# Moving two of eight depthwise-convolution tiles from TensorE to VectorE in a decoder step, with one spill and the mask conversions on other engines

## The chip, the core and the metric

The kernel runs on one core of a Trainium2 chip. The metric is the device time of one execution in microseconds (us). The core has four engines that compute: TensorE (PE in the rows, with its weight loads as PEld), VectorE (DVE), ScalarE (ACT) and GpSimd (POOL). SyncE (SP) issues transfers only; ScalarE and GpSimd issue transfers too, each from its own instruction queue. Each queue runs in order.

## What is computed

Two independent token streams pass the same two-layer trunk: a prompt of 512 tokens and a sample batch of 8 x 4 tokens. Only the prompt's part of the first layer is touched by the larger part of the change:

```python
a, g = split(h @ pw1_w + pw1_b, 2)          # D = 1024 channels
u = a * sigmoid(g)
full = concatenate([zeros(30, D), u])       # conv_prev is zero for the prompt
y = depthwise_conv(full, dw_w) + dw_b       # 31 taps for each channel, T = 512
y = silu(layer_norm(y)) @ pw2_w
```

After it come a squared-ReLU MLP, a K/V projection of the residual, stick-breaking attention (its causal mask is strict) and a second MLP. The sample goes through the same layers with a paged cache of 2048 past tokens.

## The kernel before

The prompt is held channel-major: 8 tiles of 128 channels x 512 tokens (index `kt` or `k`). Each dense product is made of three matmuls on a split of both operands into a rounded part and a rest (`whi`, `wlo` for weights, made by `wsplit`: ScalarE casts `whi` at L305, VectorE subtracts `wlo` at L306; two buffers each). The sample's dense products stream 1 MB weight blocks through four ring buffers, eight short matmul records to a block; its blocks are loaded from SP's queue.

The two streams are Python generators, `sample()` and `prompt()`. A loop at the end traces whichever has the smaller clock. Each yield adds a cost: a convolution tile 5.0 (`CV_COST`), a sample block 2.9 (`SMP_COST`); the sample starts at -20 (`CLK0`). A planner then gives each engine its fixed order: among the instructions that it takes to be ready it puts the one traced first ahead, by durations of its own; transposes and statistics of the norms (`Norm.add`) are moved ahead of others by 100 places.

The part around the change:

- The loop over `c` (four weight chunks) and `i` makes the gated tile `u` for `kt = 2c + i`: 48 matmuls, a sigmoid on ScalarE (L781), then `u` on VectorE (L785). GpSimd's queue writes `u` to the buffer `ud` in device memory behind 30 zero columns (L786); ScalarE copies the last 30 columns (L787). In the same loop the sample's gated tile and its own convolution (`sconv`, L705 and L707) run on VectorE, and the ada blocks of the sample (`early`, four to a tile from `c = 1`) on TensorE.
- `conv_load(k)` (L665) reads `ud[k]` back four times, shifted by one token each, into the 128 partitions of `raw[k]` (two buffers, four transfers of 270 KB from GpSimd's queue). The first two loads are traced in the loop above; `conv(k)` traces the load of `k + 2`.
- `conv(k)` makes `wk` on VectorE (L669), runs 32 matmuls of 128 x 32 in four column groups (L675; 64 records for a tile in the trace), adds the bias on ScalarE (L677) and gives the tile to the norm: four transposes (L351) and four statistics (L353).
- `prompt()` begins with the eight `conv(k)`, each with its yield of 5.0. Then the norm over all 1024 channels needs all eight tiles.
- `make_ax(v, 1, axd[1])`, after the first MLP, writes 8 scaled residual tiles on ScalarE (L469, in `tmp` buffers, of which there are four) and spills each to device memory from SP's queue (L471). It is traced just ahead of the K projection. The residual is read back after attention.
- Ahead of it the two attention masks are converted to bf16 in 8 copies of 64 x 128 on GpSimd (L1232); `maskx` needs a transfer of the causal tile (L1228). Attention reads the masks first at 1041.9 us.

Of the kernel before, what the change touches and what calls it, by code (L numbers as in the profile page):

```python
# [8 lines left out]
F32 = mybir.dt.float32  # L9
# [4 lines left out]
ALU = mybir.AluOpType  # L14
# [31 lines left out]
KTB = 2  # L46
STB = 3
LN_PRI = 100
CIN = 0
EIN = 4  # L50
CV_COST = 5.0
LN_COST = 16.0
# [59 lines left out]
def yoco_step_kernel(  # L112
# [353 lines left out]
    def make_ax(n, i, spill=None):  # L466
        for k in range(KT):
            t = n[k] if spill is None else tmp("axs")
            order(act(t, n[k], AF.Identity, scale=aln[:, i, k : k + 1], bias=aln[:, 4 + i, k : k + 1]), latest_act[-1])  # L469
            if spill is not None:  # L470
                dma(spill[k], t)  # L471

    def load_ax(i, k):
        t = tmp("axl")
# [184 lines left out]
    cnrm = Norm()  # L659
    raw = {}  # L660

    def conv_load(k):
        raw[k] = pld.tile([P, 4, T + 28], F32, tag="ur", bufs=2, name="ur")
        for j in range(4):
            pdma(raw[k][32 * j : 32 * j + 32], ud[k].rearrange("(g c) t -> c g t", g=4)[:, :, j : j + T + 28])  # L665

    def conv(k):
        wk = pld.tile([P, 32, 32], F32, tag="wk", bufs=2, name="wk")
        vec.tensor_tensor(wk, sel4.unsqueeze(1).to_broadcast([P, 32, 32]),  # L669
                          wtap[:, k, :].unsqueeze(2).to_broadcast([P, 32, 32]), op=ALU.mult)  # L670
        for ts in parts(H_CV and k == KT - 1):
            a = pm("cv")[:, 0 : ts.stop - ts.start]
            for m in range(8):
                for g in range(4):
                    mm(a[32 * g : 32 * g + 32, :], wk[:, 8 * g + m, :], raw[k][:, g, 4 * m + ts.start : 4 * m + ts.stop],  # L675
                       start=(m == 0), stop=(m == 7), tile_position=(0, 32 * g))
            act(y[k][:, ts], a, AF.Identity, bias=pcol(R_DWB, k))  # L677
            cnrm.add(y[k], k, ts)
        if k + 2 < KT:
            conv_load(k + 2)  # L680

    sy = sfm("sy", "sv", 2)

# [36 lines left out]
    for c in range(4):  # L720
# [48 lines left out]
        for i in range(2):  # L769
            kt = 2 * c + i  # L770
            if c:
                ws = [wsplit(st[o], i * P, P) for o in range(2)]
                accs = [pm("pw1") for _ in range(2)]
                for a, (whi, wlo) in zip(accs, ws):
                    for k in range(KT):
                        mm3(a, whi[:, k, :], wlo[:, k, :], hhi[k], hlo[k], k == 0, k == KT - 1)
                acc = accs
            else:
                acc = accs[2 * i : 2 * i + 2]
            sg = tmp("sg")  # L780
            act(sg, acc[1], AF.Sigmoid, bias=pcol(R_PWB + 1, kt))  # L781
            for _ in itertools.islice(early, EIN if c else 0):
                pass
            u = tmp("u")
            vec.scalar_tensor_tensor(u, acc[0], pcol(R_PWB, kt), sg, op0=ALU.add, op1=ALU.mult)  # L785
            pdma(ud[kt][:, CW - 1 : T + CW - 1], u)  # L786
            nc.scalar.copy(utail[:, kt, 0 : CW - 1], u[:, T - CW + 1 : T])  # L787
            if kt < 2:
                conv_load(kt)
            if kt < CIN:  # L790
                conv(kt)

    bq = base.tile([P, 8], F32, name="bq")
    for g in range(4):
# [361 lines left out]

    def prompt():

        for k in range(CIN, KT):
            conv(k)  # L1160
            yield CV_COST
        crow_ = ring("ucrow")[0:32, 0:D]
        for c in range(2):
# [65 lines left out]
        for t, src in ((maskw, ident), (maskx, causal)):  # L1229
            for hf in range(2):  # L1230
                for o in range(2):
                    nc.gpsimd.tensor_copy(t[hf * 64 : hf * 64 + 64, o, :], src[(hf ^ o) * 64 : (hf ^ o) * 64 + 64, :])  # L1232
        make_ax(v, 1, axd[1])
        kd = dr.tile([KT, P, T], F32, name="kd")
        vd = dr.tile([T, D], F32, name="vd")
# [212 lines left out]
```

## Time and profile before

| what | value |
|---|---|
| time, median of three runs | 1698.54 us (1697.76 to 1699.73) |
| the profiled execution | 1699.24 us |
| its span in the trace | 1697.5 us |
| TensorE busy | 1582.7 us, 93% of the span |
| VectorE busy | 918.8 us, 54% |
| ScalarE busy | 565.2 us, 33% |
| GpSimd busy | 196.0 us, 12% |
| convolution matmuls (L675) | 182 to 277 us of the span |

The profiled execution's time is 1.7 us longer than the span of its trace, and 0.7 us above the median of the runs. Busy times of TensorE are those of pipelined matmuls, so neighbouring records overlap, and a fully busy stretch need not be one at peak rate. A row of the timeline merges neighbours of one kind; in square brackets stand the idle time of the engine before it and what ended that.

### The profile page before, as it was taken

The numbers are of one execution on the slowest core, as the hardware profiler recorded it, in microseconds if no ns is written. First come the engines' busy times: TensorE is split into PE (matmuls) and PEld (weight loads), VectorE is DVE, ScalarE is ACT, GpSimd is POOL, SyncE is SP. The second block draws the span as 40 slices with busy tenths as digits, with TensorE's granted clock in tenths as the row PEclk, the third lists the DMA queues.
The fourth block names the chain that finished last, engine by engine and source line by source line (L and its number), as shares of the span: only waits on it lengthen the run. The fifth ranks groups of instructions, "written<-read, shape, count | busy, mean of one in ns | idle before, by whom it ended". The sixth has DMA issues, their size and how long they took to land.

```text
span 1697.5 us, 25694 instructions
## 1 busy us (share of the span) xinstructions
PE 1582.7 (93%) x10617; PEld 1095.9 (65%) x10617; DVE 918.8 (54%) x1744; ACT 565.2 (33%) x903; POOL 196.0 (12%) x239
## 2 busy tenths in 40 slices
PE   5899987989999999999989998988979999999995
PEld 2566422655777777777557865555767767557885
DVE  2465424566576655655563455986675434324446
ACT  1322103326222322333162253754172333223332
POOL 4110110100111211110011201021101000000002
PEclk9899999999999999999999999999999999999998
DMA  9798778969766866586879967364646495993221
GB/s 287 247 292 320 225 224 314 369 215 366 243 239 229 329 231 238 177 313 229 298 277 336 318 235 279 138 225 146 218 165 228 170 354 216 352 335 130 82 73 50
DMA packets 153769, 412.00 MB, mean 243 GB/s; under 512 B 8967, under 2 KB 82983, under 8 KB 129061
## 3 DMA queue, kind: packets, MB, share of 16 engines
q1 hardware_dynamic: 49891, 161.86, 26.1%
q0 software_dynamic: 24384, 151.81, 24.7%
q10 hardware_dynamic: 79378, 96.70, 17.4%
q8 instruction: 83, 1.36, 0.3%
q14 instruction: 33, 0.27, 0.1%
HBM read 392.78 MB, written 18.41 MB: 242 GB/s over the span
## 4 chain that ended last, share of the span: by engine, by line
PE 70%; issue 13%; DMA 9%; DVE 5%; ACT 2%; POOL 1%; ACTq 0%; DVEq 0%; POOLq 0%
PE pd L312 16%; PE pd L316 16%; PE pd L315 15%; PE cv L675 2%; PE sd_acc L536 2%; PE av L1029 2%; DMA kraw<-in_cache_k_dram,krow 2%; PE zt L978 2%; DMA stage<-in_conv_pw_w_dram 2%; PE pw L312 2%; PE pw L316 2%; PE pw L315 2%; DMA vt<-in_cache_v_dram,vrow 2%; DMA sw<-in_mlp_w_dram 2%; PE w_acc L563 1%
## 5 line engine op out<-in xcount | busy, mean ns | idle before, releaser
L306 DVE TENSOR_TENSOR wlo<-stage,whi 128x1024 fp32r<-128x1024 f32 x184 | 223.7, 1220 | 247.5 <-ACT whi L305 246.3
L305 ACT CAST whi<-stage 128x1024 fp32r<-128x1024 f32 x184 | 191.8, 1046 | 453.0 <-PE pd L316 378.9
L312 PE MATMUL pd<-xhi,whi 128*128 128x512 f32 (+1 forms) x832 | 317.8, 383 | 8.9 <-ACT whi L305 5.5
L315 PE MATMUL pd<-xhi,wlo 128*128 128x512 f32 (+1 forms) x832 | 315.4, 381 | 5.0 <-DVE wlo L306 4.6
L316 PE MATMUL pd<-xlo,whi 128*128 128x512 f32 (+1 forms) x832 | 309.3, 382 | 5.6 <-DVE xlo L445 4.4
L972 DVE STREAM_TRANSPOSE kt<-kraw 128x512 f32<-128x512 f32 x256 | 163.8, 686 | 104.4 <-DMA kraw<-in_cache_k_dram,krow 64.9
L312 PE MATMUL pd<-h2h,whi 128*128 128x512 f32 (+1 forms) x544 | 207.5, 388 | 2.1 <-DVE v L1147 1.6
L315 PE MATMUL pd<-h2h,wlo 128*128 128x512 f32 (+1 forms) x544 | 205.8, 382 | 0.0
L316 PE MATMUL pd<-h2l,whi 128*128 128x512 f32 (+1 forms) x544 | 204.6, 383 | 0.0
L312 PEld LDWEIGHTS pd<-xhi,whi 128*128 128x128 f32 x832 | 158.1, 190 | 59.7 <-ACT whi L305 14.8
L316 PEld LDWEIGHTS pd<-xlo,whi 128*128 128x128 f32 x832 | 155.0, 190 | 52.5 <-DVE xlo L445 9.7
L315 PEld LDWEIGHTS pd<-xhi,wlo 128*128 128x128 f32 x832 | 158.1, 190 | 46.1 <-issue 11.0
L1147 DVE SCALAR_TENSOR_TENSOR v<-pd,mod_B,v 128x512 f32<-128x512 f32 x120 | 87.2, 743 | 138.7 <-PE pd L316 138.3
L950 POOL DMA_INDIRECT kraw<-in_cache_k_dram,krow x64 | 65.7, 1026 | 604.4 <-DVE kt L972 404.7
L312 PEld LDWEIGHTS pd<-h2h,whi 128*128 128x128 f32 x544 | 102.0, 188 | 39.0 <-issue 12.1
L315 PEld LDWEIGHTS pd<-h2h,wlo 128*128 128x128 f32 x544 | 102.2, 188 | 28.4 <-issue 9.0
L316 PEld LDWEIGHTS pd<-h2l,whi 128*128 128x128 f32 x544 | 101.9, 188 | 26.5 <-issue 8.1
L1122 ACT ACTIVATE relu<-pd 128x512 f32<-128x512 f32 (+1 forms) x68 | 39.0, 573 | 236.2 <-PE pd L316 236.2
L950 POOL DMA_INDIRECT vt<-in_cache_v_dram,vrow x64 | 67.7, 1057 | 213.7 <-PE av L1029 176.2
L978 PE MATMUL zt<-kt,qb 128*32 128x128 f32 x2048 | 78.2, 280 | 9.2 <-DVE kt L972 8.4
L978 PEld LDWEIGHTS zt<-kt,qb 128*32 128x32 f32 x2048 | 53.8, 110 | 34.8 <-issue 17.9
L353 DVE BATCH_NORM_STATS2 bn<-lnT 128x6 f32<-128x128 f32 x160 | 36.6, 285 | 66.5 <-PE lnT L351 66.3
(295 smaller groups left out, 2015.7 us busy)
## 6 DMA issues: line engine op xcount, KB each, us to landing
sw<-in_mlp_w_dram SPq DMA_DIRECT2D x64, 1024.0 KB
stage<-in_mlp_w_dram ACTq DMA_DIRECT2D x64, 1024.0 KB
adaw<-in_ada_w_dram SPq DMA_DIRECT2D x40, 1024.0 KB
stage<-in_conv_pw_w_dram ACTq DMA_DIRECT2D x12, 1024.0 KB
ur<-ud POOLq DMA_DIRECT2D x32, 270.0 KB, 6.5
adaw<-in_ada_w_dram SPq DMA_DIRECT2D x16, 512.0 KB
swkv<-in_w_kv_dram SPq DMA_DIRECT2D x8, 1024.0 KB
stage<-in_w_kv_dram ACTq DMA_DIRECT2D x8, 1024.0 KB
```

Source lines behind the costliest of these rows:

```text
L305: nc.scalar.copy(hi, st[:, :, c0 : c0 + cw])
L306: vec.tensor_tensor(lo, st[:, :, c0 : c0 + cw], hi.bitcast(F32), op=ALU.subtract)
L312: first = mm(out, whi, xh, start=start, stop=False)
L315: mm(out, wlo, xh, start=False, stop=False)
L316: latest[:] = [mm(out, whi, xl, start=False, stop=stop)]
L353: vec.bn_stats(self.st[:, i, k, :], pt[:, i * P : i * P + P])
L536: mm(acc[32 * g : 32 * g + 32, :], hT[:, kk * 2 + kp, :], blk[:, kp * D + c * 512 : kp * D + c * 512 + 512], start=(kk == 0), stop=(kk == ...
L950: nc.gpsimd.indirect_dma_start(out=out, out_offset=None, in_=cache.rearrange("g (r e) h d -> (g r) (e h d)", e=2), in_offset=bass.Indirect ...
L972: ins = vec.transpose(kt[:, 2 * x : 2 * x + 2, :], raw[x].rearrange("p (e c) -> p e c", e=2)[:, :, c0 : c0 + 256])
L978: behind(mm(zt[u][32 * g : 32 * g + 32, f * P : f * P + P], qb[:, u, hh * 8 + bl].rearrange("p x q -> p (x q)"), kt[:, :, bl * 32 : bl * 3 ...
L1122: latest_act[:] = [act(r, a, AF.Relu)]
L1147: ins = vec.scalar_tensor_tensor(v[kt][:, ts], a, gt[:, kt, 8:9], v[kt][:, ts], op0=ALU.mult, op1=ALU.add)
```

## The change

Channel tiles 0 and 2 (`TAPS`) no longer go through `ud`, `conv_load` and TensorE. Their `u` is written by VectorE into a padded buffer `upad` in on-chip memory behind 30 zeroed columns. ScalarE makes tap 0 with the bias (`act`), and VectorE adds taps 1 to 30 one by one in place: 30 `scalar_tensor_tensor` instructions of 128 x 512 for a tile, each reading what the one before wrote. The tile then goes to the norm as before. The taps are a generator: five are traced behind each of the eight `u` tiles, and six behind each `conv(k)` of the six remaining tiles, until all 60 are out. The loads of `raw` follow the list of the six remaining tiles. `prompt()` yields its 5.0 six times in place of eight.

The spill of the residual (L471) is issued from ScalarE's queue in place of SP's. The 8 mask copies run on VectorE in place of GpSimd.

```diff
--- before.py
+++ after.py
@@ -46,7 +46,6 @@
 KTB = 2
 STB = 3
 LN_PRI = 100
-CIN = 0
 EIN = 4
 CV_COST = 5.0
 LN_COST = 16.0
@@ -468,7 +467,7 @@
             t = n[k] if spill is None else tmp("axs")
             order(act(t, n[k], AF.Identity, scale=aln[:, i, k : k + 1], bias=aln[:, 4 + i, k : k + 1]), latest_act[-1])
             if spill is not None:
-                dma(spill[k], t)
+                nc.scalar.dma_start(spill[k], t)
 
     def load_ax(i, k):
         t = tmp("axl")
@@ -659,6 +658,25 @@
     cnrm = Norm()
     raw = {}
 
+
+    TAPS = (0, 2)
+    REST = [k for k in range(KT) if k not in TAPS]
+    upad = {}
+
+    def conv_taps(k):
+        up = upad[k]
+        act(y[k], up[:, 0:T], AF.Identity, scale=prm[:, R_DW, k : k + 1], bias=pcol(R_DWB, k))
+        for j in range(1, CW):
+            vec.scalar_tensor_tensor(y[k], up[:, j : j + T], prm[:, R_DW + j, k : k + 1], y[k], op0=ALU.mult, op1=ALU.add)
+            yield
+        cnrm.add(y[k], k, ALL)
+
+    taps = itertools.chain(*[conv_taps(k) for k in TAPS])
+
+    def some_taps(n):
+        for _ in itertools.islice(taps, n):
+            pass
+
     def conv_load(k):
         raw[k] = pld.tile([P, 4, T + 28], F32, tag="ur", bufs=2, name="ur")
         for j in range(4):
@@ -676,8 +694,8 @@
                        start=(m == 0), stop=(m == 7), tile_position=(0, 32 * g))
             act(y[k][:, ts], a, AF.Identity, bias=pcol(R_DWB, k))
             cnrm.add(y[k], k, ts)
-        if k + 2 < KT:
-            conv_load(k + 2)
+        if k in REST[:-2]:
+            conv_load(REST[REST.index(k) + 2])
 
     sy = sfm("sy", "sv", 2)
 
@@ -781,14 +799,19 @@
             act(sg, acc[1], AF.Sigmoid, bias=pcol(R_PWB + 1, kt))
             for _ in itertools.islice(early, EIN if c else 0):
                 pass
-            u = tmp("u")
+            if kt in TAPS:
+                upad[kt] = pld.tile([P, T + CW], F32, tag="upad", bufs=len(TAPS), name="upad")
+                vec.memset(upad[kt][:, 0 : CW - 1], 0.0)
+                u = upad[kt][:, CW - 1 : T + CW - 1]
+            else:
+                u = tmp("u")
             vec.scalar_tensor_tensor(u, acc[0], pcol(R_PWB, kt), sg, op0=ALU.add, op1=ALU.mult)
-            pdma(ud[kt][:, CW - 1 : T + CW - 1], u)
+            if kt not in TAPS:
+                pdma(ud[kt][:, CW - 1 : T + CW - 1], u)
             nc.scalar.copy(utail[:, kt, 0 : CW - 1], u[:, T - CW + 1 : T])
-            if kt < 2:
+            if kt in REST[:2]:
                 conv_load(kt)
-            if kt < CIN:
-                conv(kt)
+            some_taps(5)
 
     bq = base.tile([P, 8], F32, name="bq")
     for g in range(4):
@@ -1156,8 +1179,9 @@
 
     def prompt():
 
-        for k in range(CIN, KT):
+        for k in REST:
             conv(k)
+            some_taps(99 if k == REST[-1] else 6)
             yield CV_COST
         crow_ = ring("ucrow")[0:32, 0:D]
         for c in range(2):
@@ -1229,7 +1253,7 @@
         for t, src in ((maskw, ident), (maskx, causal)):
             for hf in range(2):
                 for o in range(2):
-                    nc.gpsimd.tensor_copy(t[hf * 64 : hf * 64 + 64, o, :], src[(hf ^ o) * 64 : (hf ^ o) * 64 + 64, :])
+                    vec.tensor_copy(t[hf * 64 : hf * 64 + 64, o, :], src[(hf ^ o) * 64 : (hf ^ o) * 64 + 64, :])
         make_ax(v, 1, axd[1])
         kd = dr.tile([KT, P, T], F32, name="kd")
         vd = dr.tile([T, D], F32, name="vd")
```

## Rows read from the trace of the kernel before

**Rows 1.** The page: busy time by engine, and the chain that ended last.
```profile
PE 1582.7 (93%) x10617; PEld 1095.9 (65%) x10617; DVE 918.8 (54%) x1744; ACT 565.2 (33%) x903; POOL 196.0 (12%) x239
...
PE 70%; issue 13%; DMA 9%; DVE 5%; ACT 2%; POOL 1%; ACTq 0%; DVEq 0%; POOLq 0%
```

**Rows 2.** Two stretches: length, busy PE, PEld, DVE, ACT, POOL; granted clock, DMA share, GB/s.
```profile
85.00:182.00 97.00, 94.91 (x564) 66.83 (x563) 54.36 (x104) 22.01 (x40) 8.22 (x15) 0.98 0.88 302
182.00:279.00 97.00, 87.77 (x698) 27.52 (x697) 27.67 (x79) 10.20 (x17) 13.66 (x25) 0.96 0.79 239
```

**Rows 3.** The chain in order of time (start us, us, what), convolution matmuls.
```profile
182.22 6.15 PE cv L675 x56
...
188.71 5.27 PE cv L675 x42
```

**Rows 4.** TensorE's groups by line, 180 to 280 us: busy us, mean ns | idle before.
```profile
L675 PE MATMUL cv<-ur,wk 128*32 128x512 f32 x512 | 66.0, 611 | 4.5 <-DMA ur<-ud 4.5
L563 PE MATMUL w_acc<-sw,hT 128*32 128x512 f32 x112 | 16.5, 631 | 4.8 <-DMA sw<-in_mlp_w_dram 4.8
```

**Rows 5.** VectorE's groups by line and shape, whole span.
```profile
L1010 DVE SCALAR_TENSOR_TENSOR z_s<-z_s,fc,fx 128x512 f32<-128x512 f32 x16 | 11.3, 747 | 0.1
```

**Rows 6.** VectorE's timeline, two instructions of which the second reads the first.
```profile
287.00 0.68 DVE L405 TENSOR_TENSOR v<-v,mb 128x512 f32<-128x512 f32 x1
287.71 0.69 DVE L406 TENSOR_TENSOR v<-v,rb 128x512 f32<-128x512 f32 x1
```

**Rows 7.** Timelines of VectorE, then ScalarE, around the fifth and the seventh gated tile.
```profile
140.21 1.23 DVE L306 TENSOR_TENSOR wlo<-stage,whi 128x1024 fp32r<-128x1024 f32 x1 [0.18 <-ACT whi L305]
...
171.58 0.75 DVE L785 SCALAR_TENSOR_TENSOR u<-pw,prm,sg 128x512 f32<-128x512 f32 x1
172.24 1.22 DVE L306 TENSOR_TENSOR wlo<-stage,whi 128x1024 fp32r<-128x1024 f32 x1
...
146.43 1.06 ACT L305 CAST whi<-stage 128x1024 fp32r<-128x1024 f32 x1 [6.14 <-PE pw L316]
...
176.21 1.05 ACT L305 CAST whi<-stage 128x1024 fp32r<-128x1024 f32 x1 [3.63 <-PE pw L316]
```

**Rows 8.** Timelines of ScalarE and then SP's queue at the residual spill.
```profile
869.43 2.22 ACT L469 ACTIVATE axs<-v,aln 128x512 f32<-128x512 f32 x3
873.25 1.99 ACT L305 CAST whi<-stage 128x1024 fp32r<-128x1024 f32 x2 [1.60 <-PE pd L316]
...
876.72 0.41 ACTq L298 DMA_DIRECT2D stage<-in_w_kv_dram  x1
...
879.44 0.59 ACT L1242 COPY kT<-pd 128x512 f32<-128x512 f32 x1 [0.46 <-DMA axd<-axs]
...
870.26 9.06 SPq L471 DMA_DIRECT2D axd<-axs  x8
880.05 0.32 SPq L1243 DMA_DIRECT2D kd<-kT  x1
```

**Rows 9.** GpSimd's timeline around the mask copies.
```profile
840.29 1.36 POOL L1232 CAST maskw<-c 64x128 bf16<-64x128 f32 x4 [71.99 <-PE pd L316]
849.75 0.96 POOL L950 DMA_INDIRECT kraw<-in_cache_k_dram,krow  x1 [8.11 <-PE ada_A L238]
```

**Rows 10.** VectorE's copies of like size, by line, whole span.
```profile
L695 DVE COPY sfull<-stT 128x120 f32<-128x120 f32 x16 | 3.3, 276 | 3.8 <-PE stT L692 3.8
```

**Rows 11.** A group of VectorE's at the kernel's end; GpSimd's timeline beside it.
```profile
L1392 DVE SCALAR_TENSOR_TENSOR yt<-yt,mv,gb 128x512 f32<-128x512 f32 x4 | 6.0, 1544 | 0.0
...
1682.99 4.61 POOL L1390 TENSOR_TENSOR yt<-yt,gb 128x512 f32<-128x512 f32 x3
```

**Rows 12.** VectorE's and GpSimd's timelines at a load of the convolution's input.
```profile
189.77 1.23 DVE L669 TENSOR_TENSOR wk<-c,wtap 128x1024 f32<-128x1024 f32 x1 [0.17 <-PE cv L675]
...
190.03 2.21 POOL L665 DMA_DIRECT2D ur<-ud  x4 [5.60 <-PE cv L675]
```

**Rows 13.** Waits of SP's queue, 180 to 300 us: total, times, longest.
```profile
SPq L561 <- PE sd_acc L536: 30.6, 3, 29.7
```

## Prediction

> **What bounds the kernel now.** I read the page's busy times and the chain first, then the two stretches that the change touches, then single rows. TensorE is busy for 93% of the span and carries 70% of the chain that ended last; VectorE is busy for 54% [rows 1]. So time is gained where TensorE work leaves and nothing later takes its place. While the gated tiles are made (85 to 182 us) TensorE is busy for 94.9 of 97 us and VectorE for 54.4; in the convolution (182 to 279 us) it is 87.8 of 97 against 27.7 [rows 2]. The chain runs through the convolution's matmuls themselves [rows 3], so they are on the path. The 9.2 us that TensorE is not busy there are two waits for transfers: 4.5 us for a refill of the convolution's input and 4.8 us for the sample's weight blocks [rows 4].
>
> **What the change takes from TensorE.** 56 records of a convolution tile took 6.15 us and 42 took 5.27 us [rows 3], 98 in 11.42 us or 0.1165 us each; 64 make a tile, 7.46 us. Busy time would say 66.0 / 8 = 8.25 us [rows 4], but neighbouring records overlap. I take 7.46: two tiles are 14.9 us off the path (16.5 at most). The transposes for the norm stay. With the tiles go two yields of 5.0: when the last convolution tile is traced, the sample has been given (20 + 30) / 2.9 = 17.2 blocks in place of (20 + 40) / 2.9 = 20.7. These 3.4 blocks, 1.2 us of TensorE each (16.5 us for 112 records, eight to a block, [rows 4]), are not saved; they fall into later stretches. So the convolution should become shorter by about 14.9 + 4 = 19 us, and the kernel by 14.9 before costs. The transfers lose two writes of 256 KB and eight reads of 270 KB, 2.6 MB, and GpSimd's queue ten issues; nothing waits for that queue otherwise, so I count no gain, but it is the reason to keep open that the 9.3 us of waits shrink.
>
> **What the change adds on VectorE.** An instruction of the taps' kind and shape with all operands in on-chip memory took 747 ns [rows 5]. Each tap reads the one before; such a pair started 0.71 us apart for a first instruction of 0.68 us [rows 6], 0.03 more than its length. So a tap is 0.78 us, 60 are 47 us, five are 3.9 us. The two `wk` that go (1.23 us each, [rows 12]) are 2.5 us less. In the first stretch 40 taps take 31 us of VectorE's 42.6 free ones, in the second 20 take 15.6 of 69 [rows 2]: there is room. The last 20 are traced behind the first four of six tiles, so the last tap should be done two tiles ahead of the norm. Room on average is not cover at each place, though. What is queued behind five taps is the next `wlo`, which TensorE waits for: it was traced later, so the planner puts the taps ahead. The tightest of the six such places: `u` at 171.58, `wlo` from 172.24 to 173.46; it is wanted when the accumulation ahead of it ends, at 176.21, where the next cast is released [rows 7]. That is a margin of 2.7 us against 3.9 us of taps: 1.2 us late. The next tightest of the other five is `wlo` ready at 141.44 and wanted at 146.43 [rows 7], 5.0 us, which covers the burst. Cost taken: 1.2 us; between nothing, if the planner starts `wlo` first, and 6 us, if the later places slip by as much each. Tap 0 on ScalarE replaces the bias on ScalarE: nothing, since ScalarE is busy for 10 of 97 us there [rows 2].
>
> **The spill.** SP's eight issues sit between 870.26 and 879.3 us, each waiting for its tile; what follows on SP's queue at 880.05 waits for `kT`, not for them [rows 8]. So SP's queue gives nothing back. On ScalarE each issue takes some 0.41 us (the weight load at 876.72), eight are 3.3 us, in a stretch where ScalarE runs from the spilled tiles to the casts of the next weights and to `kT` without much rest [rows 8]; behind the issues wait those casts, for which TensorE waits in turn. Three tiles with three issues fit ahead of the cast of 873.25, which TensorE releases: 869.43 + 2.22 + 1.2 = 872.9. The other five issues lie ahead of `kT` and delay it by up to 2 us. I take 1.0 us, between 0 and 3.3. The Trainium skill says in "DMA: Bandwidth & Descriptors", section "Issuing engines are not separate DMA queues", that transfers issued from different engines share the same DMA engines, so that another issuer saves the issue time alone; by that the move has nothing to gain in landing times, and with all of the issue time on the path the sum would be 1688.6. No row here shows the spill from the other queue.
>
> **The masks.** On GpSimd the first four took 1.36 us after a wait of 72 us, and what stood behind them, a gather at 849.75, waited for a ring buffer [rows 9]; so GpSimd's queue held nothing up. On VectorE, copies of like size took 0.28 us [rows 10], eight 2.2 us, at the norm ahead of the K projection, where TensorE waits for VectorE. They are traced behind the norm and fill gaps of its chain; I take 0.5 us, between 0 and 2.2. The masks are needed at attention, long after.
>
> **Sum.** 1699.24 - 14.9 + 1.2 + 1.0 + 0.5 = 1687.0 for an execution like the profiled one, which is 0.7 us above the median of the runs: 1686.
>
> **The rivals.**
> A, the sample's chain starts late. Five taps behind the last `u` and six behind the first convolution tile are traced ahead of, or among, the sample's small dependent VectorE steps at 185 to 209 us. 11 x 0.78 = 8.6 us later would be the matmuls that free the ring, for which the first block of the sample's MLP waits (SP's longest wait there is 29.7 us, [rows 13]); TensorE, in order, then waits in front of a block. For it: both transfer waits of this stretch are of that family [rows 4]. Against: those steps were traced before the convolution's taps, so only five taps lie ahead for sure, and TensorE has convolution tiles to fill with. It leaves 1686 + 8.6 = 1695. The planner putting the 20 late taps at the end of the convolution, so that the norm waits, comes out about there too.
> B, the waits go. With 2.2 MB less of refills in the convolution both waits of 9.3 us vanish: 1686 - 9.3 = 1677. For it: a refill is what the 4.5 us waited for [rows 4]. Against: six tiles in less time ask for the four refills that are left at the same pace as before, and the mean share of the transfers is 0.79 already [rows 2].
> C, slower: VectorE becomes the bound of the first stretch. At the end of the kernel four instructions of this very kind and shape took 1.54 us each on average, while GpSimd computed beside them [rows 11]; the 747 ns are from where it does not. At 1.54 us 40 taps with their gaps are 63 us on top of 54.4: 117 for 97, 20 more, and 1686 + 20 = 1706. It decides from a tap with its gap of (97 + 14.9 - 54.4) / 40 = 1.44 us on; from (97 - 54.4) / 40 = 1.07 to there it only eats the gain. Against: GpSimd does nothing but issue transfers there, and an instruction with two on-chip operands beside such an issue kept its 1.23 us [rows 12]. The Trainium skill states in "SBUF — State Buffer", section "Who interferes with whom", that a VectorE instruction with two such inputs contends with a GpSimd instruction that reads this memory; rows 11 agree, and rows 12 show no such thing for an issue.
>
> **How the numbers follow.** Forecast as summed 0.50, B 0.15, A 0.17, C 0.08. The last 0.10 is a redrawn plan: every engine's order is laid out anew once the sample runs 3.4 blocks later, the norms then have other work beside them, and no row prices that; I give half of it to no change and half to slower. A change of 0.2%, 3.4 us, is about what a measurement of this kernel can tell from none; faster then ends at 1695.1, where A lies, so A counts half as faster. Faster is 0.50 + 0.15 + 0.08 = 0.73, the same 0.09 + 0.05 = 0.14, slower 0.08 + 0.05 = 0.13. The range runs from B with no costs (1699.24 - 14.9 - 9.3 - 0.7 = 1674) to A with the upper bounds of the two costs on ScalarE and at `wlo` on top: 1695 + (6 - 1.2) + (3.3 - 1.0) = 1702. C lies outside.
>
> **What would show it.** In the changed kernel's profile: 384 records of the convolution in place of 512, 60 taps of about 0.75 us with starts 0.78 apart, the convolution some 19 us shorter, TensorE's busy sum some 15 us down, and its waits for `wlo` between 85 and 182 us at 1 to 2 us. A tap of over 1 us speaks for C; a convolution stretch shorter by only 10 us with longer waits for the sample's blocks or for the norm's transposes speaks for A; no transfer waits there for B. At 870 to 885 us TensorE's waits for the casts and for free accumulators tell the spill's price. I am wrong if the stretch gives its 15 us and later stretches take them back, which would show as TensorE idle elsewhere, above all at the norms.

## The result, and the profile after

The changed kernel takes 1680.28 us (median, 1679.56 to 1684.09) where the kernel before took 1698.91 beside it: a ratio of 0.9896, with a 95% interval of 0.988 to 0.9912. That is 18.6 us less where 12.2 were forecast, and inside the range. The profiled execution took 1680.33 us with a span of 1678.6, 18.9 below the 1697.5 of before.

The page of the changed kernel, busy times and the chain that ended last (before: [rows 1]):

```profile
PE 1568.0 (93%) x10489; PEld 1091.6 (65%) x10489; DVE 955.8 (57%) x1812; ACT 570.0 (34%) x903; POOL 186.6 (11%) x221
...
PE 79%; DVE 8%; DMA 6%; issue 5%; ACT 2%; POOL 0%; ACTq 0%; SPq 0%; DVEq 0%; POOLq 0%
```

TensorE is busy for 14.7 us less. That is not the two tiles alone: the convolution's own records were busy for 66.0 us before [rows 4] and for 49.2 after, 16.8 less, and all the others together for 2.1 more. (Two executions with the same records differ by as much: the kernel with the masks alone, below, whose time is that of the kernel before, was profiled with 1578.6 us of busy time, 4.1 less.) The other 4.2 of the 18.9 us are idle time of TensorE (1697.5 - 1582.7 = 114.8 before, 1678.6 - 1568.0 = 110.6 after). But that small difference hides large ones. The windows below cut both traces at the same events: the last gated tile, the last convolution eviction, the last residual of the second pointwise layer, the last MLP tile, the first and the last eviction of K. Columns are as in [rows 2]; before first, then after:

```profile
182.80:277.30 94.50, 85.27 (x678) 26.70 (x674) 27.25 (x78) 8.84 (x17) 13.66 (x25) 0.96 0.80 240
277.30:371.30 94.00, 81.58 (x492) 50.43 (x484) 56.53 (x161) 29.05 (x43) 4.35 (x8) 0.97 0.84 310
371.30:840.30 469.00, 465.03 (x3224) 337.40 (x3225) 285.22 (x488) 157.00 (x239) 58.49 (x57) 1.00 0.71 260
840.30:879.40 39.10, 31.01 (x166) 17.87 (x165) 29.53 (x71) 22.54 (x32) 6.13 (x12) 0.96 0.79 291
879.40:984.80 105.40, 103.06 (x887) 85.33 (x886) 40.53 (x61) 34.13 (x48) 17.16 (x16) 0.99 0.88 311
```

```profile
181.90:246.70 64.80, 59.80 (x501) 20.46 (x502) 24.23 (x76) 6.30 (x11) 9.30 (x17) 0.97 0.71 216
246.70:337.90 91.20, 85.98 (x518) 51.40 (x510) 52.14 (x130) 30.05 (x45) 4.35 (x8) 0.96 0.89 338
337.90:810.50 472.60, 465.46 (x3214) 339.92 (x3217) 290.86 (x520) 158.73 (x237) 57.96 (x56) 0.99 0.71 256
810.50:861.30 50.80, 37.24 (x204) 19.31 (x203) 32.27 (x80) 24.50 (x34) 4.51 (x4) 0.94 0.99 369
861.30:964.70 103.40, 99.39 (x846) 82.41 (x846) 33.94 (x46) 30.53 (x43) 14.16 (x14) 0.98 0.79 282
```

Read down the lengths: the convolution loses 29.7 us, the stretch behind it 2.8 more, the MLP gives back 3.6 (mostly idle time, 7.1 us for 4.0, which no run here explains), and the lead-in to K gives back 11.7 (5.5 of it idle time, 6.2 busy with 38 more records). At the last eviction of K the changed kernel is 20.1 us ahead, at the end 18.9. So the change won 33 us by the end of the second pointwise layer and lost some 15 of them before K. Two questions follow: why the first number is so much larger than 14.9, and what happens at K.

**The taps.** VectorE's group of taps by line and shape, a burst and the last tap from its timeline, and the first stretch's window:

```profile
L670 DVE SCALAR_TENSOR_TENSOR v<-upad,prm,v 128x512 f32<-128x512 f32 x60 | 43.4, 791 | 0.0
...
156.39 7.44 DVE L670 SCALAR_TENSOR_TENSOR v<-upad,prm,v 128x512 f32<-128x512 f32 x11
179.23 0.80 DVE L670 SCALAR_TENSOR_TENSOR v<-upad,prm,v 128x512 f32<-128x512 f32 x1
...
85.00:182.00 97.00, 94.97 (x562) 64.46 (x554) 95.72 (x171) 23.53 (x42) 7.18 (x13) 1.00 0.86 298
```

All sixty are over at 180 us, ahead of all but 8 of the convolution's records: the planner put them into VectorE's gaps of the first stretch and left VectorE 1.3 us of rest in 97. Eleven taps in 7.44 us are one every 0.67 us, (7.44 - 0.75) / 10.

**The convolution.** TensorE's groups by line from 180 to 250 us (before: [rows 4]), and, from its timeline, its one long wait for VectorE in the first stretch:

```profile
L693 PE MATMUL cv<-ur,wk 128*32 128x512 f32 x376 | 48.1, 615 | 5.0 <-DMA ur<-ud 5.0
L562 PE MATMUL w_acc<-sw,hT 128*32 128x512 f32 x64 | 9.3, 595 | 0.0
...
139.92 0.50 PE L314 MATMUL pw<-xhi,wlo 128*128 128x512 f32 x1 [1.76 <-DVE wlo L305]
```

The wait for the refill stays (5.0 us, 4.5 before), the one for the sample's weight blocks is gone from here (4.8 before). Of the sample, 52 `w_acc` records start ahead of the convolution's last eviction, where 92 did before: 40 fewer, five blocks.

**The hole at K.** TensorE's wait at the first transposes of K, which the kernel before does not have; then ScalarE's timeline up to the first K eviction, and GpSimd's:

```profile
PE kn L1271 <- ACT kT L1266: 7.2, 1, 7.2
...
840.40 1.51 ACT L468 ACTIVATE axs<-v,aln 128x512 f32<-128x512 f32 x2
841.81 0.80 ACT L468 ACTIVATE axs<-v,aln 128x512 f32<-128x512 f32 x1
846.87 1.99 ACT L304 CAST whi<-stage 128x1024 fp32r<-128x1024 f32 x2 [4.26 <-PE pd L315]
851.23 0.82 ACT L468 ACTIVATE axs<-v,aln 128x512 f32<-128x512 f32 x1 [1.89 <-DVE maskx L1256]
857.52 0.81 ACT L468 ACTIVATE axs<-v,aln 128x512 f32<-128x512 f32 x1 [1.67 <-DMA axd<-axs]
861.34 0.59 ACT L1266 COPY kT<-pd 128x512 f32<-128x512 f32 x1 [3.00 <-DMA axd<-axs]
...
837.46 0.98 POOL L973 DMA_INDIRECT kraw<-in_cache_k_dram,krow  x1 [82.57 <-PE ada_A L237]
848.37 1.63 POOL L973 DMA_INDIRECT vt<-in_cache_v_dram,vrow  x1 [0.71 <-PE ada_A L237]
```

The spilled tiles (`axs`) come from the four rotating temporaries, `tmp`, and so do the causal mask's source and the evicted K tile. Before, eight spilled tiles went out in 10 us [rows 8]; here they take from 840.4 to 858.3. The fourth waits for the mask copies (`maskx`), which hold the temporary of the causal source; the eighth, and then K's eviction, wait for a spill to land. At the same time the sample's four gathers of cache rows are issued, 837.5 to 848.4; before, they came from 849.75 [rows 9] to 863.9 us, ahead of the spills at 869.4. What the gathers' queue moved around the spills, before (866 to 881 us) and after (838 to 862), from the views of the transfers (packets, MB, share of the 16 engines):

```profile
q0 software_dynamic: 135, 0.96, 17.7%
```

```profile
q0 software_dynamic: 576, 4.19, 53.7%
```

The same view of the changed kernel in finer windows, the gathers' queue from 850 to 854 us and ScalarE's from 858 to 860:

```profile
q0 software_dynamic: 182, 1.35, 97.4%
...
q10 hardware_dynamic: 648, 0.79, 107.5%
```

So the last spills stand behind two things: the gathers, whose last bytes move between 856 and 858 us, and a weight block of 1 MB that ScalarE issued at 852.54 us, between the fourth spill and the fifth. K's eviction still waits at 861 us, when the gathers are over.

### The profile page after: what moved, and what is told of

Read it like the earlier page. It is cut to its first block, busy times and chain, and to the rows that moved or that the text cites. A ratio compares the mean times of both kernels' runs of the same rounds, so it can differ in the third digit from the quotient of the medians.

```text
span 1678.6 us, 25451 instructions
## 1 busy us (share of the span) xinstructions
PE 1568.0 (93%) x10489; PEld 1091.6 (65%) x10489; DVE 955.8 (57%) x1812; ACT 570.0 (34%) x903; POOL 186.6 (11%) x221
## 4 chain that ended last, share of the span: by engine, by line
PE 79%; DVE 8%; DMA 6%; issue 5%; ACT 2%; POOL 0%; ACTq 0%; SPq 0%; DVEq 0%; POOLq 0%
PE pd L311 18%; PE pd L315 18%; PE pd L314 18%; PE zt L1001 4%; PE av L1052 3%; PE sd_acc L535 2%; PE cv L693 2%; DMA stage<-in_conv_pw_w_dram 2%; PE w_acc L562 1%; DVE v L670 1%; PE ada_A L237 1%; PE lnT L350 1%; PE pv L1288 1%; PE pv L1290 1%; PE pv L1289 1%
## 5 line engine op out<-in xcount | busy, mean ns | idle before, releaser
L311 PE MATMUL pd<-xhi,whi 128*128 128x512 f32 (+1 forms) x832 | 322.7, 389 | 9.5 <-ACT whi L304 5.2
L314 PE MATMUL pd<-xhi,wlo 128*128 128x512 f32 (+1 forms) x832 | 319.3, 385 | 2.9 <-DVE wlo L305 2.7
L315 PE MATMUL pd<-xlo,whi 128*128 128x512 f32 (+1 forms) x832 | 313.1, 386 | 5.6 <-DVE xlo L444 5.4
L311 PEld LDWEIGHTS pd<-xhi,whi 128*128 128x128 f32 x832 | 161.7, 194 | 60.1 <-issue 13.7
L314 PEld LDWEIGHTS pd<-xhi,wlo 128*128 128x128 f32 x832 | 161.6, 194 | 42.9 <-issue 11.8
L1001 PEld LDWEIGHTS zt<-kt,qb 128*32 128x32 f32 x2048 | 53.3, 111 | 30.6 <-issue 15.3
```

The source lines that it names most:

```text
L311: first = mm(out, whi, xh, start=start, stop=False)
L314: mm(out, wlo, xh, start=False, stop=False)
L315: latest[:] = [mm(out, whi, xl, start=False, stop=stop)]
L1001: behind(mm(zt[u][32 * g : 32 * g + 32, f * P : f * P + P], qb[:, u, hh * 8 + bl].rearrange("p x q -> p (x q)"), kt[:, :, bl * 32 : bl * 3 ...
```

## The experiments

Two things were to be explained: the first stretches' extra gain, and the hole. Ratios are against the kernel before, run beside each.

**Parts of the change alone.** The first theory (H): the second and third part of the change make the hole, since they put the spills' issues and the mask copies on engines that K waits for. The rival (S): the sample's later place makes it.

The convolution's part alone. Against the changed kernel:

```
-                nc.scalar.dma_start(spill[k], t)
+                dma(spill[k], t)
...
-                    vec.tensor_copy(t[hf * 64 : hf * 64 + 64, o, :], ...)
+                    nc.gpsimd.tensor_copy(t[hf * 64 : hf * 64 + 64, o, :], ...)
```

> Two tiles tap by tap as in the change; the spill stays on SP's queue and the masks on GpSimd. Theory H (the spill and the masks together make the hole of 7.25 us in front of the K projection's first transposes in the changed kernel): the hole goes, 1672 to 1675 us. Rival S (the hole comes from the sample's blocks that lie elsewhere once the convolution is shorter): the hole stays, 1679 to 1682 us.

Measured: 1687.63 us, 0.9941 (0.9921 to 0.9961). Neither theory had that. The hole is there, and larger; TensorE's wait, GpSimd's timeline, then ScalarE's, and the windows of the hole and of the 5 us behind it:

```profile
PE kn L1271 <- ACT kT L1266: 11.8, 1, 11.8
...
858.50 0.98 POOL L1256 CAST maskx<-causal 64x128 bf16<-64x128 f32 x3 [7.08 <-DMA vt<-in_cache_v_dram,vrow]
...
866.33 0.81 ACT L468 ACTIVATE axs<-v,aln 128x512 f32<-128x512 f32 x1 [2.96 <-DMA axd<-axs]
...
856.00:867.00 11.00, 0.00 (x0) 0.00 (x0) 1.23 (x1) 4.53 (x6) 0.88 (x3) 0.60 0.60 188
867.00:872.00 5.00, 4.33 (x13) 3.60 (x14) 0.00 (x0) 1.70 (x4) 0.00 (x0) 0.51 0.69 247
```

H falls: the convolution's part alone brings the hole, and the other two parts together make it smaller. On GpSimd the last three mask copies come at 858.5, behind a wait of 7.08 us for a gather's transfer; the fourth spilled tile waits for them. The eighth then waits 2.96 us for a spill to land, though no byte of the gathers moves after 858 us; a weight block issued at 859.57 us is on its way by then.

The spill alone on the kernel before:

```
-                dma(spill[k], t)
+                nc.scalar.dma_start(spill[k], t)
```

> The kernel before with the spill alone on ScalarE's queue. If the issues on ScalarE's queue alone make the hole: 1703 to 1707 us. If the hole needs the masks on VectorE too (they free the causal tile's buffer, for which a spilled tile waits): 1698 to 1701 us. By my prediction's own price: 1.0 us more, 1700 us.

Measured: 1700.44 us, 1.0017 (1.0000 to 1.0033). In its trace K's first eviction starts at 879.47 us, before at 879.44 [rows 8]: the issues run beside ScalarE's own arithmetic and hold up nothing there.

The masks alone on the kernel before:

```
-                    nc.gpsimd.tensor_copy(t[hf * 64 : hf * 64 + 64, o, :], ...)
+                    vec.tensor_copy(t[hf * 64 : hf * 64 + 64, o, :], ...)
```

> The kernel before with the mask copies alone on VectorE. By my prediction's own price 0.5 us more, 1699.4 us. If the late copies of the causal tile on VectorE hold the buffer wherever the spill is issued: 1702 to 1706 us, with the residual tiles stretched over more than 12 us as in the changed kernel.

Measured: 1698.63 us, 1.0000 (0.9988 to 1.0013).

The convolution and the spill, with the masks left on GpSimd:

> Two tiles tap by tap and the spill on ScalarE's queue; the masks stay on GpSimd. If the spill alone makes the hole: as the changed kernel, 1679 to 1682 us. If it needs the masks on VectorE: 1672 to 1675 us.

Measured: 1687.98 us, 0.9930 (0.9904 to 0.9956), and the hole is 12.0 us. So the spill's new queue is worth nothing that shows, alone or with the rest. The Trainium skill states in "DMA: Bandwidth & Descriptors", section "Issuing engines are not separate DMA queues", that transfers started by different engines run on the same DMA engines and that issuing from several saves the issue time alone. This case agrees: 1.0000 to 1.0033. The masks' move is worth nothing alone, but within the change the ratio goes from 0.9930 to 0.9896 with it (the two intervals just overlap) and the hole from 12.0 to 7.25 us.

**The causal source.** The next theory (N): the hole is the temporary that the causal source holds until the mask copies have run. The edit, on three kernels:

```
-        causal = tmp("causal")[:, 0:P]
+        causal = pl3.tile([P, P], F32, name="causal")
```

On the changed kernel:

> The changed kernel whole, with one edit: the causal mask's source, which stood in one of the four rotating temporaries, gets a tile of its own. Theory N (the hole of 7.25 us ahead of the first transposes of the K projection is this temporary: it is held until the four mask copies have run, so that the spilled tiles and the first K eviction share three buffers, and the copies stand behind other work on their engine): the hole falls to 1 us or less, the eight spilled tiles end by 849 us instead of 858.3, and the time is 1680.3 - 7.2 = 1673, within 2 us. Rival R (the hole is the later place of the sample's work, which keeps ScalarE, VectorE and the weights late there; the temporary is only where the wait shows): the hole moves to another wait and the time stays between 1679 and 1682.

Measured: 1682.31 us, 0.9917 (0.9896 to 0.9939), next to the rival's range, and the hole is still 6.8 us. Why N missed is in ScalarE's timeline:

```profile
853.98 0.39 ACTq L297 DMA_DIRECT2D stage<-in_w_kv_dram  x1
854.42 1.52 ACT L468 ACTIVATE axs<-v,aln 128x512 f32<-128x512 f32 x2 [2.62 <-DVE wlo L305]
...
863.36 0.58 ACT L1266 COPY kT<-pd 128x512 f32<-128x512 f32 x1 [5.05 <-DMA axd<-axs]
```

The second four spilled tiles now stand behind the issue of a weight load, which waits for its buffer; then K's eviction waits 5.05 us for one of them to land, all four temporaries being on their way to memory. One wait was taken away and the next took its place.

On the convolution's part alone:

> The convolution's part of the change alone (spill on the sync queue, mask copies on GpSimd), with the causal mask's source in a tile of its own. Theory N: the hole of 11.83 us falls to 1 us or less and the time is 1687.6 - 11.5 = 1676, within 2.5 us; then the mask copies' engine is worth nothing by itself. Rival R: the copies on GpSimd still come behind the sample's gathers, the masks are wanted only later, and the time stays at 1686 to 1689.

Measured: 1679.01 us, 0.9891 (0.9867 to 0.9914); the hole fell from 11.8 to 5.6 us. The time is 0.5 us above N's range and 7 below the rival's, but the hole is only halved, in a profile of the longest of the four executions (1685.58 us). With the source in its own tile and the masks left on GpSimd the ratio is that of the whole change (0.9896). So the third part of the change seems to do just this: it sets the temporary free earlier.

On the kernel before:

> The kernel before with only the causal mask's source in a tile of its own. Theory N: the kernel before has no hole at the K projection, so nothing is won: 1698, within 1.5 us, ratio 0.999 to 1.001. Rival: the temporary cost the kernel before something too, at a place that the idle times ahead of the K projection do not show: 1695 or less.

Measured: 1695.16 us, 0.9991 (0.9976 to 1.0006): nothing, as N had it.

**The price of the taps.**

```
     for j in range(1, CW):
         vec.scalar_tensor_tensor(ytap[k], up[:, j : j + T], prm[:, R_DW + j, k : k + 1], ytap[k], ...)
...
-            u = tmp("u")
+            if kt in TAPS:
...
+            some_taps(5)
```

> The kernel before with the sixty taps added as extra work: two tiles are convolved on VectorE into scratch tiles that nobody reads, at the same places in the program, while TensorE still convolves all eight. It shows the price of the taps without their gain. My forecast put that price at 1.2 us (the low halves of the weight stages late behind bursts of five taps): 1699 to 1700. Rival C, reduced (VectorE is full in the first stretch, 80.0 of 80 us, so that the taps hold up more than the 1.8 us that waits for the low halves show): 1702 to 1706. A third reading (the taps fill idle time only): 1697.5 to 1698.5.

Measured: 1703.13 us, 1.0035 (1.0018 to 1.0052), so 3 to 9 us for sixty taps. But the trace doesn't show where: the taps stand as in the changed kernel (87.0 to 180.4 us), no wait of TensorE for VectorE above 0.4 us between 85 and 182 us, the convolution's last eviction at 276.7 us (277.3 before), the span 2.5 us longer. The price is above my 1.2; its place stays open.

**The spills.** Theory G: the temporaries come free late because the spills are written beside the gathers. One run takes away the temporaries, one the gathers.

The spilled tiles scaled in place, so that they need no temporary. (Q's input is made from the same tiles later and gets scaled values in this kernel; the work is the same.)

```
-            t = n[k] if spill is None else tmp("axs")
+            t = n[k]
```

> The changed kernel with one edit: the eight spilled tiles are scaled in place in the norm's own tiles and written from there, so that they take none of the four rotating temporaries. Theory G (the temporaries come free late since the spills are written slowly: the four gathers of the sample's cache rows, 4.19 MB on GpSimd's queue, are issued at 837.5 to 848.4 us, on top of the spills, and ScalarE's first K eviction waits for a spill to land): the hole ahead of the first K transposes falls from 7.25 us to 1 us or less, K's first eviction comes by 855 us instead of 861.3, and the time is 1680.3 - 6.5 = 1674, within 2 us. Rival R (the temporaries are only where it shows; what is late is the DMA engines as such, and the K stores or weights will show it instead): the time stays at 1679 to 1682.

Measured: 1673.45 us, 0.9851 (0.9824 to 0.9878), G's value. The gathers stand where they stood (839.2 to 850.2 us) and the hole is gone; K's first eviction, and the windows of the lead-in and of K:

```profile
848.65 0.59 ACT L1266 COPY kT<-pd 128x512 f32<-128x512 f32 x1 [0.71 <-PE pd L315]
...
811.70:848.60 36.90, 28.60 (x172) 14.15 (x166) 27.42 (x75) 20.63 (x30) 2.04 (x3) 1.00 0.99 373
848.60:957.30 108.70, 104.86 (x880) 85.80 (x878) 38.85 (x51) 34.27 (x48) 17.68 (x16) 1.00 0.87 315
```

The lead-in is 36.9 us in place of 50.8; 5.3 of those 13.9 come back in K's stretch, which now holds 34 records more (880 for 846), where the lead-in holds 32 fewer (172 for 204).

The other side: the gathers back ahead of the spills, by a higher planned cost of a convolution tile.

```
-CV_COST = 5.0
+CV_COST = 40.0 / 6
```

> The changed kernel with the planner's cost of a convolution tile raised from 5 to 6.67, so that the six tiles carry as much of the sample's work as the eight did before. It tells what the sample's later place is worth. Theory G: the gathers come again 5 to 20 us ahead of the spills and the hole falls from 7.25 us to 2 us or less. If the sample's place is neutral otherwise, the convolution's stretch ends some 12 us later than in the changed kernel, the later stretches get that back, and the time is 1674 to 1676. If the later place had filled idle time at the norms behind the convolution (idle there: 11.3 us before, 8.9 us after the change), that comes back, and the time is 1677 to 1680. Rival (the hole does not hang on where the sample stands): hole of 6 us or more, 1680 or above.

Measured: 1679.38 us, 0.9870 (0.9840 to 0.9900). The gathers come at 831 to 845.5 us, 5 to 20 us ahead of the spills at 851, and TensorE shows no wait for K's eviction. The hole is gone from this side too. That does not show the gathers alone to be the reason: the weight block stands otherwise as well here, behind the fifth spill (858.75 us), and the convolution's part alone had a wait for a spill with no gather beside it. Gathers and weight block were not taken apart. As to the time, four executions from 1674.14 to 1682.02 us and an interval that holds both 0.9851 and 0.9896 do not tell 1674 from 1680. The profile, of the longest of them, shows something that could cost time: the transfers around the spills, the stretch behind the convolution and TensorE's longest wait in it.

```profile
q0 software_dynamic: 123, 0.88, 12.8%
...
246.30:351.60 105.30, 88.13 (x536) 53.90 (x528) 57.27 (x162) 30.51 (x45) 4.34 (x8) 0.92 0.89 339
...
PE smp L499 <- DVE sred L497: 7.6, 2, 5.9
```

That stretch is 14.1 us longer than in the changed kernel, and TensorE idles for 17.2 us of it (105.30 - 88.13) in place of 5.2. So the sample's later place seems to have had two effects: work left over for the norms behind the convolution (7.2 us less idle time there in the changed kernel than before), and gathers on top of the spills. By this one profile the kernel here gives up the first to be rid of the second. Wrong was my expectation that the convolution itself would grow by 12 us: it is as short as in the changed kernel (64.6 us), and the sample's new pace shows only behind it.

**A third tile**, on top of the spills in place (and with the same scaled values in Q's input):

```
-    TAPS = (0, 2)
+    TAPS = (0, 2, 4)
```

> As the first kernel of this call (spills in place), with three tiles on VectorE instead of two: 90 taps. TensorE loses a third convolution tile of 7.46 us and the planner another 5 of cost. If VectorE has room for 30 more taps of 0.67 us (20 us): 1674 - 7.5 = 1666.5, within 2.5 us. Rival C (VectorE, busy 80.0 of 80 us in the first stretch, bounds it with three tiles: the remaining taps stand in one burst at the end of the first stretch and hold up the weights' low halves, the convolution's filters and the norm): the last tap comes later than 190 us, TensorE waits for VectorE more than 8 us there, and the time is 1673 to 1685.

Measured: 1681.12 us, 0.9873 (0.9837 to 0.9910): in the median 7.7 us slower than with two, with intervals that overlap, and far from the 1666.5 of a third gain. By the time it is the rival's case. VectorE's timeline at the end of the taps, TensorE's longest wait from 230 to 285 us, and the window of that stretch:

```profile
241.87 15.71 DVE L670 SCALAR_TENSOR_TENSOR v<-upad,prm,v 128x512 f32<-128x512 f32 x20
...
PE w_acc L562 <- DMA sw<-in_mlp_w_dram: 9.3, 6, 2.7
...
237.00:285.00 48.00, 34.81 (x190) 13.56 (x190) 43.39 (x92) 18.64 (x30) 0.92 (x2) 0.79 0.84 323
```

The first stretch was full with sixty. The last twenty taps stand in one burst behind the convolution, up to 257.6 us, and the norm's statistics of that tile come after them (259.82). TensorE has only the sample's blocks meanwhile, waits for their weights (the 8 us of waits for VectorE that the rival named are not there), and is idle for 13.2 of 48 us at a mean granted clock of 0.79. But that VectorE has no room for a third tile is not shown. ScalarE's tap 0 of that tile, and the window of the convolution:

```profile
222.79 0.80 ACT L668 ACTIVATE v<-upad,prm 128x512 f32<-128x512 f32 x1
...
182.00:237.00 55.00, 50.72 (x394) 17.72 (x393) 25.68 (x73) 7.04 (x12) 7.12 (x13) 0.94 0.62 184
```

Beside the convolution VectorE had 29.3 us free, and thirty taps of 0.67 us are 20. The program as written traces the third tile late: its tap 0 and four taps behind the fourth convolution tile, the other 26 behind the fifth and last. A version that traces them earlier was not run.

**A version faster than both.** The residual's spill moved to the V projection, one tile behind each of its eight steps, with the rest of the change kept:

```
-        make_ax(v, 1, axd[1])
...
                 dma(nv_out[:, 2 * i2 : 2 * i2 + 2, c * 256 : c * 256 + 256], tv)
+                make_ax(v, 1, axd[1], [2 * c + i2])
```

> The changed kernel with the spill of the residual moved: not all eight tiles ahead of the K projection, but one behind each of the eight steps of the V projection, where the norm's tiles are still whole (Q's input is made from them only later). The output is the reference's, unlike with the scaling in place, which hands scaled tiles to Q. Theory G (eight spills at once fill the four temporaries, and these come free only when the spills have landed beside the gathers): the hole ahead of the first K transposes (7.25 us) and the low clock behind it are gone, each V step takes two temporaries of four in some 5 us, which shows no wait above 0.5 us, and the time is that of the scaling in place, 1673.5, within 2.5 us. Rival (the spills meet the next gathers in the V projection, and the evictions there wait for temporaries, one at a time): waits of 1 us or more at several V steps, 1677 to 1683.

Measured: 1673.21 us, 0.9855 (0.9835 to 0.9876). TensorE's waits from 840 to 965 us and the windows of the lead-in and of K:

```profile
PE pd L311 <- ACT whi L304: 3.2, 3, 2.0
PE pd L315 <- DVE xlo L444: 1.7, 1, 1.7
PE kn L1270 <- ACT kT L1265: 1.0, 1, 1.0
...
812.70:849.00 36.30, 28.68 (x172) 14.22 (x172) 27.46 (x75) 14.96 (x22) 2.06 (x3) 1.00 0.98 378
849.00:956.90 107.90, 103.17 (x879) 85.75 (x878) 39.04 (x51) 38.95 (x54) 16.71 (x16) 0.99 0.89 315
```

The hole is down to 1.0 us. The spills, from 904.8 to 958.2 us, meet no wait for a temporary above 0.5 us. The 2.0 us behind the end of V are in the changed kernel too (2.0 at the same line). The 1.7 us are not: ScalarE makes the eighth spilled tile there (957.40 us) ahead of the next operands, so one of the moved spills seems to cost that. The rival's waits at several V steps did not come. The interval lies below that of the changed kernel (0.988 to 0.9912).

## Why the prediction was right, and where its steps were not

- **Two tiles off TensorE, 14.9 us.** Right: 384 records of the convolution are left of 512. That the whole busy sum fell by 14.7 is luck as a check on the 14.9: 16.8 went in the convolution, near the 16.5 that I had set aside for busy time, and 2.1 came back in other records.
- **The convolution 19 us shorter.** Wrong in size: 29.7. The step counted 14.9 for the tiles and 4 for 3.4 blocks of the sample. Five blocks left the stretch, 40 records of 16.5 / 112 us [rows 4], 5.9 us; TensorE's idle time there fell by 4.2 us, from 9.2 to 5.0; and 14 records of the convolution run ahead of the last gated tile where 8 did (0.7 us at 0.1165). 14.9 + 5.9 + 4.2 + 0.7 = 25.7. With 16.5 for the two tiles, which the busy time gives and which I had set aside, it is 27.3; some 2 us stay unassigned.
- **The moved blocks cost later what they save here.** This step failed, on both sides. They found idle time to fill: TensorE idles for 5.2 us behind the convolution in place of 12.4. And with the sample later the gathers and a weight block came ahead of the spills' landings, and the lead-in to K grew by 11.7 us, 5.5 of it idle. The working had priced the blocks by TensorE's time alone. I left a chance of 0.10 for a redrawn plan and counted it only as harm.
- **A tap every 0.78 us.** Too long: 0.67 in a burst, 43.4 us in all for 47. The pair of [rows 6] gave start to start a length plus 0.03; a chain of taps starts each before the one ahead is recorded as ended.
- **Forty taps in the first stretch, twenty beside the convolution.** Wrong place: all sixty before it. The sum of room was right, if barely: 54.4 + 43.4 - 2.5 = 95.3 of 97, and 95.7 were measured.
- **`wlo` late by 1.2 us.** Right in kind, wrong in place. The one wait, 1.8 us up to 139.92, comes behind the fifth gated tile, which I held covered by 5.0 us; behind the seventh, the tightest by my reading, there is none. 2.8 of the 5.0 us were 24 records of the sample's ada blocks, which stood on TensorE there (from 142.26 us); after the change none stand there. The wait stands behind two taps, not five. What sixty taps cost without the gain was 3 to 9 us, more than this wait.
- **The spill's issues, 1.0 us.** They cost nothing that the trace shows, since issue and arithmetic run side by side on ScalarE; the ratio alone is 1.0000 to 1.0033.
- **The masks, 0.5 us, and "needed at attention, long after".** The price was right for the kernel before (0.9988 to 1.0013), but the reason was wrong. I asked when the masks are read. What mattered was when their source's buffer is wanted back, and that was at once: by the spills. In the changed kernel the same move is worth the difference between 0.9930 and 0.9896.
- **The rivals.** C did not come with two tiles: taps were recorded with 0.79 us on average and GpSimd did nothing but issue beside them. With three, VectorE's last taps did hold up the norm, but they were traced late, behind free time of VectorE, and they were not slower. B came in half: the wait for the refill stayed at 5.0 us, the one for the sample's blocks left the stretch, but 3.8 us of it turned up behind the convolution. A did not come; no tap stood in the sample's way.
- **The sum.** It was 6.4 us short of the gain. I had 2.7 us of costs, and idle time fell by 4.2 us instead; whatever the taps, the spill and the masks cost (sixty taps alone 3 to 9 us) is inside that balance. That this comes out so close is partly luck: by the end of the second pointwise layer the kernel was 33.4 us ahead, 14 more than the 19 I had seen coming, and of these it lost 15.3 up to K, 11 more than the 4 I had.

Open: where the taps' 3 to 9 us go when nothing is taken from TensorE; whether the gathers or the weight block keep the spills from landing; and whether a third tile gains when its taps are traced earlier.

## What to carry to other kernels

Where two streams of work are interleaved by a plan, taking work from the one moves the other against it; look which bursts of transfers come to stand together then, not only which engine is freed. A buffer in a small rotating pool is due when the pool wants it back, not when its reader's result is needed; a burst of writes through such a pool waits for the landings, so spread it, or write from tiles that are idle anyway. And when VectorE takes over TensorE's work, count the free time ahead of the point where the result is wanted, and look whether the program offers the work while that time is free: two tiles filled the gaps ahead of the convolution here, and the third came too late for those beside it.

## What the hardware showed that I had not expected

**A chain of dependent taps overlaps.** Each tap reads the tile that the one before writes, and still eleven took 7.44 us, a start every 0.67 us, while a single one is recorded with 0.75 to 0.80 us. What bounds that rate was not tried.

**A hole costs more than its length.** In the changed kernel the granted clock behind the 7.25 us hole was 0.65 on the mean of 5 us, and K's matmuls took 0.63 us where they take 0.39; TensorE's timeline, then the windows of the 5 us behind the hole and the next 5:

```profile
863.32 0.63 PE L314 MATMUL pd<-xhi,wlo 128*128 128x512 f32 x1
865.95 0.39 PE L315 MATMUL pd<-xlo,whi 128*128 128x512 f32 x1
...
862.00:867.00 5.00, 5.00 (x17) 4.17 (x18) 0.00 (x0) 1.07 (x2) 0.00 (x0) 0.65 0.49 170
867.00:872.00 5.00, 5.00 (x26) 4.12 (x25) 0.41 (x1) 2.02 (x3) 0.00 (x0) 1.00 0.18 57
```

Seventeen matmuls in place of 26. With the convolution's part alone, behind 11.8 us of rest, the 5 us from 867 us ran at 0.51, which is the lower level of 1.2 GHz. With the spills in place, and no hole, the granted clock is 1.00 in the lead-in and in K's stretch. These two stretches together are 145.6 us there and 154.2 in the changed kernel, with 1052 and 1050 records: 8.6 us, of which 5.4 are idle time and 3.2 busy time of TensorE. With the spills at V they are 144.2 us with 1051 records: 10.0 us, 5.2 of them idle and 4.8 busy. So in both the two stretches give back more than the 7.25 us, and some of it as shorter busy time. In the remainder of the span these two executions are 1.7 and 4.0 us longer than the changed kernel's, which no row here explains and which may be how executions differ.
